# One transfer with repeated rows in place of four small ones, for the gate's second matrix in a hybrid attention step

## The chip, the cores and the metric

The kernel runs on one core of a Trainium2 chip. The metric is the device time in microseconds of one execution. The engines are called by these names: PE is TensorE (matmuls; PEld its weight loads), DVE VectorE, ACT ScalarE, POOL GpSimd, SP SyncE. A transfer (DMA) is issued by an instruction in the queue of SP or ACT; the letter q behind an engine's name in the profile (SPq, ACTq) marks such an issue.

## The reference, cut to what matters

One layer of a decoder: a prompt of 512 tokens and eight single new tokens, width 1024. One input projection gives the columns for two mixers, gated linear attention (queries, keys and values `qa`, `ka`, `va`, output gate `ga`, and the 16 columns `za` of a low-rank forget gate) and dilated window attention (`qb`, `kb`, `vb`, `gb`). What the change touches is the forget gate:

```
log_a = jax.nn.log_sigmoid((jnp.einsum('btr,rk->btk', za, w_alpha2) + b_alpha).astype(F32)) / GATE_TEMP
```

`za` has 16 columns for each token, `w_alpha2` is the gate's second matrix (16 x 256) and `b_alpha` its bias (256). The decays `log_a` then enter a recurrence over the tokens. Both mixers' outputs are gated, joined and projected by `w_out`, added to the input and normalised.

## The kernel before, in words

All products in float32 precision that feed the projections are made of three faster ones: a matrix is split into a high part (ACT copies it into a rounded type) and a low part (DVE subtracts the high part), and the matmuls high x high, high x low, low x high are added in PSUM (`three`, `split`).

The order of the work is planned on the host. Each piece of work is a generator that yields one operation at a time; the planner (`Plan.run`, line 309) takes at each step the operation that can start first by its own table of costs (`Op`, line 84), and writes it to its engine's queue (line 371, so that nearly every row of the profile has this line). Each engine then works its queue strictly in that order. A change of one operation's engine or cost therefore moves others later on. Transfers take eight semaphores in turn, whoever issues them; a transfer waits until the one that used its semaphore before has landed.

The start is this. `dense` (line 715) runs eight warm-up matmuls on PE and then the first products: for each of eight blocks `k` of 128 input columns, and for each of two halves `u` of the tokens, three groups of weights (`ka0`, `ka1`, `qa1`) times x, three matmuls each: 18 matmuls a block. `first_loads` (line 558) issues the transfers for it: x in pieces (`x_raw`) and the weights (`raw_ka`), all on SP but the first weights, which ACT issues. `first_splits` (line 587) splits what has landed: into `xx` for x and `hi_ka`, `lo_ka` for the weights. Behind the loads of x and weights stand, on SP, `zw` (the weights of `za`), `cf` (an identity matrix and other constants), the small tables `rb_raw`, `cm`, `gn`, the table `ct_raw`, and then the weights of the next groups: `raw_qa`, `raw_qb` and so on (`weight_loads`, line 524).

After the eight blocks PE forms `ps_za`, the 16 gate columns of all tokens, with the tokens in four groups of 128 (`j`), each in its own 32 rows. `gate_decay` (line 777) copies it to `zT`, adding 1 in one row of each 32 so that a bias row can be used, and multiplies with `wz`, whose 32 rows of each group hold the second matrix and the bias: products `ps_z`, of 16 matmuls. Then come the log-sigmoid (`la`) and its running sum (`b`). PE meanwhile goes on with the group `qa0`, then `qb`, `kb` and the others. `ps_tab` is one matmul of a table of biases, `ps_l` are the many small matmuls of the recurrence (three passes, lines 885 to 904), `ps_og`, `ps_s`, `ps_pt`, `ps_pv` belong to the other parts, `ps_yf` and `ps_y` are the output projection.

`wz` before: `clear` (line 543) sets it to zero on DVE, and ACT issues four transfers of 18 rows of `wab`, the 16 rows of the matrix and the bias twice, one into each group's first 18 rows. `wab` is an input of 98 rows: the matrix six times, one below the other, then the bias twice. `zw` is cleared by POOL and gets the weights of `za` in the columns 0 to 15 of its 32. The 1 is added in row 16 of each 32, so it meets the first bias row.

Of the kernel before, what the change touches and what calls it, by code (L numbers as in the profile page):

```python
# [17 lines left out]
ALU = mybir.AluOpType  # L18
AX = mybir.AxisListType
# [177 lines left out]
class Plan:  # L197
# [15 lines left out]
    def add(self, gen, prio):  # L213
        self.seq += 1
        self.tasks.append(Task(gen, prio, self.seq))

    def mark(self, name):
        self.marks[name] += 1
# [4 lines left out]
    def free(self, *xs):  # L223
        for x in xs:
            name = x.tensor.name
            self.shares[name] = self.shares.get(name, 1) - 1
            if self.shares[name] == 0:
                last = {}
                for (_, eng), end in self.uses.pop(name, {}).items():
                    last[eng] = max(last.get(eng, 0.0), end)  # L230
                tag, (pool, t, _) = self.slot_of.pop(name)
                self.slots[tag].append((pool, t, last))
# [143 lines left out]
def trunk(ctx: ExitStack, tc: tile.TileContext, xT, xp, xs, state, ck, cv, w_in, wab, gnorm,  # L376
# [6 lines left out]
    T, V, S, G, D = (plan.engines[n] for n in ("PE", "DVE", "ACT", "POOL", "SP"))  # L383
# [10 lines left out]
    def bank(tag, name):  # L394
        return Need(tag, name, [P, 512])

    def cst(name, shape, dt=F32):
        return const.tile(shape, dt, name=name)
# [34 lines left out]
    ident = cf[:, C_ID:C_ID + P]  # L433
# [90 lines left out]
    def weight_loads():  # L524
        for g in order:
            for i in range(g.parts):
                yield from g.load(i)
# [10 lines left out]
    zw = plan.alloc(Need("t1", "zw", [P, KT, 32]))  # L538
    wz = plan.alloc(Need("t1", "wz", [P, 256]))
    one16 = cst("one16", [P, 1])  # L540
    ln_eps = cst("ln_eps", [P, 1])

    def clear():

        yield V.memset(wz, 0.0)
        yield V.memset(keep, 1.0)
        yield V.memset(keep[:, CH:CH + 1], 0.0)
        yield G.memset(zw, 0.0)
        for j in range(4):
            yield S.dma_start(wz[j * 32:j * 32 + 18], wab[80:98])  # L550


    W3 = 3 * P
# [4 lines left out]
    def first_loads():  # L558
        za = w_in[:, OFF["za"]:OFF["za"] + 16].rearrange("(k p) n -> p k n", p=P)
        for n, a, *b in FIRST:  # L560
            if n == "x":
                c = b[0] if b else slice(0, NT)
                if a % 2 == 0 and c.start == 0:
                    xraw.append((yield Need("g", f"x_raw{a}", [P, 2, NT])))
                yield D.dma_start(xraw[a // 2][:, a % 2, c], xT[a * P:(a + 1) * P, c])
            else:
                if a % 2 == 0:
                    ka_raw.append((yield Need("r", f"raw_ka{a}", [P, 2, W3])))
                rows = w_in[a * P:b[0] * P, P:P + W3]
                yield (S if a == 0 else D).dma_start(ka_raw[a // 2][:, a % 2:a % 2 + b[0] - a, :], rows.rearrange("(k p) n -> p k n", p=P))  # L570
                if a == 0:
                    nc.scalar.preload_act_table_set("natural_log_exp_and_others")
            mark("first")
        yield D.dma_start(zw[:, :, :16], za)
        mark("zw")
        yield D.dma_start(cf, c_f[:, :C_E2])
        add(weight_loads(), 14.8)
        B["rb_raw"] = yield Need("t1", "rb_raw", [64, NB, HB])
        for i in range(2):
            yield D.dma_start(B["rb_raw"][i * 32:i * 32 + 32], rel_bias[:, None, :].to_broadcast([32, NB, HB]))  # L580
        yield D.dma_start(cm_w, c_m)
        mark("const")
        yield D.dma_start(gn, gnorm)
# [131 lines left out]
    def dense():  # L715
# [16 lines left out]
        for x in ka_hl:  # L732
# [6 lines left out]
                    for k in range(KT) for j in range(TT))  # L739
        free(zw, *xraw)  # L740
        add(gate_decay(pz), 5.4)
        yield from make("ka", Need("g", "ka", [P, 2, NP]), 3)
        yield from make("qa", Need("g", "qa", [P, 2, NP]), 2)
# [33 lines left out]
    def gate_decay(pz):  # L777

        zT = yield Need("t1", "zT", [P, QN[1]])
        yield At("const")  # L780

        yield V.tensor_reduce(one16, ident.rearrange("p (j r) -> p j r", r=32)[:, :, 16], axis=AX.X, op=ALU.add)
        yield V.tensor_scalar(zT[:, :P], pz[:, :P], one16, None, op0=ALU.add)
        yield V.tensor_scalar(zT[32:64, P:], pz[32:64, P:QN[1]], one16[32:64], None, op0=ALU.add)
        free(pz)
        la = yield Need("g", "la", [P, 2 * NP + 2 * NB])
        b = yield Need("g", "b", [P, 2 * NP])
        B["b"] = b
        plan.share(b, 3)
        zp = yield Pair(*(bank(("s", "t"), f"ps_z{j}") for j in range(TT)))  # L790
        yield Batch(T.matmul(zp[j][:, m * QN[1]:m * QN[1] + QN[j]], wz[j * 32:j * 32 + 32, m * P:m * P + P], zT[j * 32:j * 32 + 32, :QN[j]],
                             start=m == 0, stop=m == 1, skip_group_check=True) for m in range(2) for j in range(TT))
        free(zT, wz)
        zv = [x[:, :2 * QN[1]].rearrange("p (m t) -> p m t", m=2) for x in zp]
        lv, bv = (x[:, :2 * NP].rearrange("p (m t) -> p m t", m=2) for x in (la, b))
        ls = la[:, 2 * NP:].rearrange("p (m b) -> p m b", m=2)
        parts_ = [(zv[j][:, :, :P], lv[:, :, j * P:j * P + P], lv[:, :, j * P:j * P + P]) for j in range(TT)]
        parts_.append((zv[1][:, :, P:], ls, la_s))
        for j in (0, 1, 4, 2, 3):
            z, o, to = parts_[j]  # L800
            if j == 1:
                yield S.activation(ls, parts_[4][0], AF.Abs)
            if j != 4:
                yield S.activation(o, z, AF.Abs)
            yield S.activation(o, o, AF.Exp, scale=-1.0)
            yield S.activation(o, o, AF.Ln, bias=1.0)
            yield V.scalar_tensor_tensor(to, z, 0.0, o, op0=ALU.min, op1=ALU.subtract)
            if j == 4:
                mark("la_s")
                continue  # L810
            if j != 1:
                free(zp[j])
            for m in range(2):
                yield V.tensor_tensor_scan(bv[:, m, j * P:j * P + P], keep, lv[:, m, j * P:j * P + P], 0.0, ALU.mult, ALU.add)
        free(zp[1], la)
        mark("b")
# [830 lines left out]
    nc.vector.memset(warm, 0.0)  # L1647
    warm_ps = plan.alloc(bank("t", "warm_ps"))
    add(clear(), 0)
    add(first_loads(), 0)  # L1650
    add(first_splits(), 1)
    add(fills(), 26.3)
# [134 lines left out]
```

## Time and profile before

| | us |
|---|---|
| median of 3 runs | 282.8 |
| the three runs | 282.8, 284.8, 282.66 |
| the profiled execution | 285.62 |
| its span, first to last instruction | 283.8 |
| PE busy | 271.1 (96% of the span) |
| DVE, ACT, POOL busy | 205.6, 155.2, 57.8 |

The span is the time between the first and the last instruction of the profiled execution; the rest of its time lies around it. Busy times of PE come from modelled ends of pipelined matmuls. In a row of the timeline stand: start, length, engine, line, operation, output <- input, shape, number of instructions, and in brackets the idle time of the engine ahead of it with what ended that. In a row of the view by windows stand: the stretch, its length, the busy time of the five engines (PE, PEld, DVE, ACT, POOL) with the number of instructions in brackets, the share of the TensorE clock that was granted, the mean busy share of the 16 DMA engines, and GB/s.

### The profile page before, as it was taken

To read this page: it belongs to the slowest core of one execution; us is meant where nothing else is said; L and a number is where in the kernel's file an instruction comes from. 1 tells how busy PE (TensorE), PEld (TensorE's weight loads), DVE (VectorE), ACT (ScalarE), POOL (GpSimd) and SP (SyncE) were. 2 spreads that over 40 slices of the span, in tenths; PEclk is the share of its full clock that TensorE was granted. 3 is DMA by queue.
4 is the path that set the end of the run, shared out by engine and by line. 5 is a ranking of instruction groups with operands and counts; after the bars stand their busy time and mean duration, and the time that the engine had idled before them with its cause. 6 is when DMAs were issued, how large, how long until landed. Compare 5 with 4: busy or idle time off the path is not lost.

```text
span 283.8 us, 7076 instructions
## 1 busy us (share of the span) xinstructions
PE 271.1 (96%) x2760; PEld 254.7 (90%) x2760; DVE 205.6 (72%) x506; ACT 155.2 (55%) x449; POOL 57.8 (20%) x72
## 2 busy tenths in 40 slices
PE   4999999999989999999999999999999999999990
PEld 1999999989979999999988998999999999998890
DVE  2851689999989993619978898164989895359575
ACT  3635664536633893538878784426399955243111
POOL 4000000000397043810024182453500000000000
PEclk9799999999979999999999999999999999999997
DMA  6993654624971789833999868779883463967721
GB/s 203 308 228 75 195 164 137 161 76 123 299 247 46 205 230 262 235 132 108 308 189 199 207 170 234 201 215 233 249 212 96 147 227 88 256 124 196 229 81 74
DMA packets 59087, 52.29 MB, mean 184 GB/s; under 512 B 12509, under 2 KB 49963, under 8 KB 59053
## 3 DMA queue, kind: packets, MB, share of 16 engines
q1 hardware_dynamic: 58801, 51.56, 67.0%
q8 instruction: 22, 0.36, 0.5%
q10 hardware_dynamic: 252, 0.27, 0.3%
q14 instruction: 12, 0.10, 0.1%
HBM read 46.26 MB, written 6.03 MB: 184 GB/s over the span
## 4 chain that ended last, share of the span: by engine, by line
PE 94%; DMA 2%; DVE 1%; issue 1%; ACT 1%; DVEq 0%
PE ps_kb L371 9%; PE ps_ga L371 8%; PE ps_gb L371 8%; PE ps_qb L371 8%; PE ps_yf L371 8%; PE ps_y L371 8%; PE ps_ka L371 5%; PE ps_qa L371 4%; PE ps_vb_f L371 4%; PE ps_va_f L371 4%; PE ps_vb L371 4%; PE ps_va L371 4%; PE ps_pt L371 3%; PE ps_pv L371 3%; PE ps_s L371 3%; PE ps_l L371 2%
## 5 line engine op out<-in xcount | busy, mean ns | idle before, releaser
L371 POOL TENSOR_TENSOR past<-past,qbc 128x256 f32<-128x256 f32 x32 | 27.0, 877 | 90.9 <-DMA past<-in_ck_dram 87.6
L371 POOL TENSOR_TENSOR vv<-vv,pb 128x256 f32<-128x256 f32 x32 | 27.6, 892 | 53.7 <-DVE ms L371 26.0
L371 ACT ACTIVATE pr<-pr,ms 128x128 f32<-128x128 f32 (+3 forms) x47 | 24.4, 537 | 5.8 <-DVE ms L371 5.6
L371 DVE CUSTOM_DVE_ANT_0 pr<-ps_s,strip 128x128 f32<-128x128 f32 (+3 forms) x32 | 14.3, 479 | 6.1 <-PE ps_s L371 5.9
L371 ACT COPY pt<-ps_pt 128x256 f32<-128x256 f32 (+3 forms) x25 | 10.4, 418 | 10.1 <-PE ps_pt L371 10.0
L371 PE MATMUL ps_ka<-xx,hi_ka 128*128 128x264 f32 (+1 forms) x64 | 13.1, 297 | 2.5 <-DVE hi_ka L371 2.5
L371 PE MATMUL ps_pt<-cf,pr 128*128 128x128 f32 x80 | 14.1, 280 | 0.0
L371 ACT ACTIVATE sg<-sg 128x264 f32<-128x264 f32 (+1 forms) x32 | 13.8, 431 | 0.3
L371 PEld LDWEIGHTS ps_ka<-xx,hi_ka 128*128 128x128 f32 x64 | 10.7, 203 | 3.3 <-ACT xx L371 3.2
L371 DVE SCALAR_TENSOR_TENSOR y<-y,ps_yt 128x256 f32<-128x256 f32 x8 | 3.0, 418 | 11.3 <-PE ps_yt L371 11.3
L371 DVE TENSOR_REDUCE lt<-past 128x16 f32<-128x1024 f32 x8 | 9.7, 1209 | 1.6 <-POOL past L371 1.6
L371 DVE TENSOR_REDUCE o_pv<-vv 128x4 f32<-128x1024 f32 x8 | 9.7, 1213 | 0.5 <-POOL vv L371 0.5
L371 PEld LDWEIGHTS ps_pt<-cf,pr 128*128 128x128 f32 x80 | 9.7, 142 | 0.4 <-issue 0.3
L371 PE MATMUL ps_ka<-xx,lo_ka 128*128 128x264 f32 (+1 forms) x32 | 9.7, 302 | 0.0
L371 PE MATMUL ps_pv<-pt,v 128*64 128x256 f32 (+1 forms) x96 | 9.5, 348 | 0.0
L371 ACT COPY feat_y<-ps_yf 128x256 f32<-128x256 f32 x8 | 3.0, 373 | 11.4 <-PE ps_yf L371 11.4
L371 DVE TENSOR_SCALAR pr<-pr,ms 128x512 f32<-128x512 f32 (+3 forms) x17 | 8.9, 523 | 0.2
L371 DVE TENSOR_TENSOR xx<-x_raw,xx 128x520 fp32r<-128x520 f32 (+2 forms) x10 | 5.7, 587 | 4.3 <-ACT xx L371 4.2
L371 PEld LDWEIGHTS ps_pv<-pt,v 128*64 128x64 f32 x96 | 6.3, 137 | 2.9
L371 PE MATMUL ps_kb<-xx,hi_kb__781 128*128 128x264 f32 (+1 forms) x32 | 8.5, 336 | 0.0
L371 ACT ACTIVATE rstd<-mv,ln_eps 128x1 f32<-128x1 f32 x4 | 1.2, 291 | 13.4 <-DVE mv L371 13.4
L371 PE MATMUL ps_s<-kp,qh 64*128 64x128 f32 (+3 forms) x64 | 8.4, 346 | 0.0
(534 smaller groups left out, 1038.6 us busy)
## 6 DMA issues: line engine op xcount, KB each, us to landing
past<-in_ck_dram SPq DMA_DIRECT2D x8, 512.0 KB
vv<-in_cv_dram SPq DMA_DIRECT2D x8, 512.0 KB
pb<-psd_s SPq DMA_DIRECT2D x16, 256.0 KB
s<-in_state_dram SPq DMA_DIRECT2D x4, 512.0 KB
qbc<-qsd SPq DMA_DIRECT2D x8, 256.0 KB
strip<-tabr SPq DMA_DIRECT2D x8, 256.0 KB
y<-in_xp_dram SPq DMA_DIRECT2D x4, 512.0 KB
x_raw<-in_xT_dram SPq DMA_DIRECT2D x6, 260.0 KB
```

The costliest lines, as they stand in the source:

```text
L371: getattr(eng.eng, op.fn)(*op.args, **op.kw)
```

## The change

The four transfers on ACT and the clearing of `wz` on DVE are taken out. `wz` is filled by one transfer on SP, between those of `zw` and `cf`: the last 32 rows of `wab` (its row 66 and on), four times by a repeat of step 0, so that all 128 rows of `wz` are written. Of these 32 rows the first 14 are the matrix's rows 2 to 15, then come the whole matrix (rows 14 to 29) and the bias twice (30 and 31). So the weights of `za` now go to the columns 14 to 29 of `zw`, the columns 0 to 13, 30 and 31 stay zero, and the 1 is added in row 30. The rows of `wz` that meet zeros add nothing. What is computed is the same.

```
     def clear():
-        yield V.memset(wz, 0.0)
         yield V.memset(keep, 1.0)
         yield V.memset(keep[:, CH:CH + 1], 0.0)
         yield G.memset(zw, 0.0)
-        for j in range(4):
-            yield S.dma_start(wz[j * 32:j * 32 + 18], wab[80:98])
...
-        yield D.dma_start(zw[:, :, :16], za)
+        yield D.dma_start(zw[:, :, 14:30], za)
+        yield D.dma_start(wz, wab[None, 66:].to_broadcast([4, 32, 256]))
         mark("zw")
         yield D.dma_start(cf, c_f[:, :C_E2])
...
-        yield V.tensor_reduce(one16, ident.rearrange("p (j r) -> p j r", r=32)[:, :, 16], axis=AX.X, op=ALU.add)
+        yield V.tensor_reduce(one16, ident.rearrange("p (j r) -> p j r", r=32)[:, :, 30], axis=AX.X, op=ALU.add)
         yield V.tensor_scalar(zT[:, :P], pz[:, :P], one16, None, op0=ALU.add)
```

The queue of ACT at the start of the program, first before and then after, each with the semaphores that an instruction waits for. DMAHW0 to DMAHW7 are the eight semaphores of the transfers; `wz` is the gate's matrix, `x_raw` and `raw_ka` are x and the first weights as loaded, `xx` and `hi_ka` their split parts.

```order
L371 DMA raw_ka_109<-in_w_in_dram 128x384
L572 ACT_TABLE_LOAD
L371 DMA wz<-in_wab_dram 18x256 [waits DVE_49]
L371 DMA wz<-in_wab_dram 18x256
L371 DMA wz<-in_wab_dram 18x256 [waits DMAHW1_49]
L371 DMA wz<-in_wab_dram 18x256 [waits DMAHW3_49]
L371 CAST xx_110<-x_raw_106 128x264
```

```order
L371 DMA raw_ka_109<-in_w_in_dram 128x384
L569 ACT_TABLE_LOAD
L371 CAST xx_110<-x_raw_106 128x264 [waits DMAHW1_49]
L371 CAST xx_110<-x_raw_106 128x256 [waits DMAHW2_49]
L371 CAST xx_110<-x_raw_106 128x264 [waits DMAHW3_49]
```

The first split of x stood behind four issues, the last two of which wait for the semaphores of earlier transfers; now it is the first to wait, for the first transfer of x.

The queue of SP over the same stretch, its first loads, before and then after:

```order
L371 DMA x_raw_106<-in_xT_dram 128x256
L371 DMA raw_ka_149<-in_w_in_dram 128x384 [waits DMAHW0_49]
L371 DMA x_raw_152<-in_xT_dram 128x520 [waits DMAHW2_49]
L371 DMA raw_ka_149<-in_w_in_dram 128x384 [waits DMAHW4_49]
L371 DMA x_raw_152<-in_xT_dram 128x520 [waits DMAHW5_49]
```

```order
L371 DMA x_raw_106<-in_xT_dram 128x256
L371 DMA raw_ka_140<-in_w_in_dram 128x384
L371 DMA x_raw_146<-in_xT_dram 128x520
L371 DMA raw_ka_140<-in_w_in_dram 128x384 [waits DMAHW0_49]
L371 DMA x_raw_146<-in_xT_dram 128x520 [waits DMAHW1_49]
```

Without the four transfers the eight semaphores last longer: SP's sixth and seventh load no longer wait, and the later ones wait for earlier transfers than they did. Behind the loads, `wz` now stands on SP between `zw` and `cf`.

The queue of ACT around the split of `raw_qa`, the weights of the group `qa0`, before and then after (`rb` is the small table's copy, `tsb` the bias table's result from `ps_tab`, `ka` the first evacuated product):

```order
L371 CAST rb<-rb_raw 64x64
L371 CAST hi_qa__327<-raw_qa__227 128x1024
L371 COPY tsb<-ps_tab 8x512
L371 ACTIVATE ka<-ps_ka_137 128x256
L371 ACTIVATE ka_s<-ps_ka_137 128x8
```

```order
L371 CAST rb<-rb_raw 64x64
L371 COPY tsb<-ps_tab 8x512
L371 CAST hi_qa__315<-raw_qa__231 128x1024
L371 ACTIVATE ka<-ps_ka_132 128x256
L371 ACTIVATE ka_s<-ps_ka_132 128x8
```

The copy of `tsb` has moved ahead of the split of `raw_qa`; on PE the matmul `ps_tab` has moved with it, from the middle of the last block to its start. Further on, between the gate's product and the first pass of `ps_l`, a dozen rows of DVE and ACT stand in another order, and single rows of PE have moved by one to some twenty places; nothing else has changed.

More of the change, by code (lines that the diff above doesn't have):

```diff
@@ L543, in clear @@
     def clear():
-        yield V.memset(wz, 0.0)
         yield V.memset(keep, 1.0)
@@ L548, in clear @@
         yield G.memset(zw, 0.0)
-        for j in range(4):
-            yield S.dma_start(wz[j * 32:j * 32 + 18], wab[80:98])
     W3 = 3 * P
@@ L573, in first_loads @@
             mark("first")
-        yield D.dma_start(zw[:, :, :16], za)
+        yield D.dma_start(zw[:, :, 14:30], za)
+        yield D.dma_start(wz, wab[None, 66:].to_broadcast([4, 32, 256]))
         mark("zw")
@@ L780, in gate_decay @@
         yield At("const")
-        yield V.tensor_reduce(one16, ident.rearrange("p (j r) -> p j r", r=32)[:, :, 16], axis=AX.X, op=ALU.add)
+        yield V.tensor_reduce(one16, ident.rearrange("p (j r) -> p j r", r=32)[:, :, 30], axis=AX.X, op=ALU.add)
         yield V.tensor_scalar(zT[:, :P], pz[:, :P], one16, None, op0=ALU.add)
```

## The prediction

> **What bounds the kernel now.** I read the page of the profile first, for the engine that carries the chain that ended last.
>
> ```profile
> span 283.8 us, 7076 instructions
> PE 94%; DMA 2%; DVE 1%; issue 1%; ACT 1%; DVEq 0%
> ```
>
> TensorE carries 94% of that chain, so this change can save only where TensorE waits or runs slowly. The two small shares left, DMA and ACT, say where to look next: the first microseconds of the chain of waits, in order of time.
>
> ```profile
> 0.73 2.73 DMA x_raw<-in_xT_dram
> ...
> 3.48 2.34 DMA wz<-in_wab_dram
> 5.82 0.41 ACT xx L371
> ...
> 6.26 0.43 DVE xx L371
> 6.69 0.28 DVE hi_ka L371
> ...
> 7.11 0.48 PE ps_ka L371 x2
> ```
>
> The columns are start, length and what ran. The first tile of x lands at 0.73 + 2.73 = 3.46 us, yet its split on ScalarE begins at 5.82. Between stand 2.34 us under the name of the table `wz`, the gate's second matrix. The timeline of ScalarE and TensorE shows what this is.
>
> ```profile
> 1.19 3.42 PE L371 MATMUL warm_ps<-warm 128*128 128x512 bf16 x8 [1.19 <-DVE warm L1647]
> 3.48 0.28 ACTq L371 DMA_DIRECT2D wz<-in_wab_dram  x1
> 5.49 0.28 ACTq L371 DMA_DIRECT2D wz<-in_wab_dram  x1
> 5.81 1.03 ACT L371 CAST xx<-x_raw 128x264 fp32r<-128x264 f32 x3 [3.35 <-DMA wz<-in_wab_dram]
> 7.11 0.48 PE L371 MATMUL ps_ka<-xx,hi_ka 128*128 128x264 f32 x2 [2.50 <-DVE hi_ka L371]
> 11.15 0.41 PE L371 MATMUL ps_ka<-xx,hi_ka 128*128 128x264 f32 x2
> 13.33 0.28 PE L371 MATMUL ps_ka<-xx,hi_ka 128*128 128x264 f32 x1
> ```
>
> The four transfers themselves are small:
>
> ```profile
> wz<-in_wab_dram ACTq DMA_DIRECT2D x4, 18.0 KB
> ```
>
> The third of them is issued only at 3.48, the fourth only at 5.49. The order's rows above say why: these two wait for the DMA semaphores DMAHW1 and DMAHW3, which the transfers of x took before them (all transfers take eight semaphores in turn). ScalarE works in order, so the split of x stands behind the issue at 5.49, though its own data had come at 3.46. TensorE, after its warm-up, stands still for 2.50 us.
>
> The same rows hold a second cost. The 18 matmuls of the first block k run from 7.11 to 11.15, 4.04 us; those of the second from 11.15 to 13.33, 2.18 us. The work is equal. The view by windows has the granted clock (the column of one number after the five engines):
>
> ```profile
> 4.30:7.70 3.40, 0.88 (x5) 0.39 (x3) 1.41 (x4) 1.89 (x6) 0.00 (x0) 1.00 0.87 246
> 7.70:11.10 3.40, 3.40 (x16) 3.40 (x17) 3.34 (x8) 1.95 (x4) 0.00 (x0) 0.50 0.98 299
> 75.99:79.40 3.41, 2.09 (x124) 1.94 (x125) 2.64 (x7) 1.42 (x7) 3.33 (x4) 1.00 1.00 371
> 79.40:82.80 3.40, 3.40 (x20) 3.33 (x20) 2.91 (x6) 1.09 (x4) 3.10 (x5) 0.50 0.83 231
> ```
>
> TensorE was busy for 0.88 of 3.40 us, and the next 3.40 us were granted at 0.50. The same comes back at 79.40, behind a stretch with 2.09 busy. So a stretch of idle is paid twice here: once as idle, once as half clock afterwards.
>
> **The change part by part.**
>
> Start of TensorE. The four issues leave ScalarE. Its first split then waits for x alone and begins at 3.48, where the third issue now stands for the same semaphore, in place of 5.81: 2.33 us. Behind it come the rows 5.82 to 7.11 unchanged, since the first weights have landed by then (SyncE issues a transfer that waits for them, DMAHW0, at 3.73, a row below). TensorE starts at 7.11 - 2.33 = 4.78, against a warm-up that ends at 1.19 + 3.42 = 4.61. First term: 2.33.
>
> Clock of the first block. The idle stretch falls from 2.50 to 0.17 us, so the stretch from 4.30 to 7.70 is nearly all busy, and by the rows above the half clock should not follow. Bounds: 0 (it follows anyway) and 4.04 - 2.18 = 1.86. I take 1.86, since 3.4 - 0.2 of 3.4 us busy is nearer to the stretches at full clock than to the 0.88 and 2.09 that were punished. The Trainium skill, page "TensorE: Matmul & The Clock Gate", Part 1, says that a free-running window of about 3.4 us of activity sets the clock, half or full, so that its phase differs from run to run; the trace agrees with the length (3.40) and the two values. By that page some of the 1.86 could remain in a run whose window ends late; the case "start only" below has what that would give.
>
> Loads under the faster start. With 2.18 us a block, block 4 begins at 4.78 + 4 x 2.18 = 13.50. It needs the splits of loads that come now at these times:
>
> ```profile
> 11.80 0.83 ACT L371 CAST hi_ka<-raw_ka 128x768 fp32r<-128x768 f32 x1 [1.18 <-DMA raw_ka<-in_w_in_dram]
> 13.54 0.69 DVE L371 TENSOR_TENSOR xx<-x_raw,xx 128x520 fp32r<-128x520 f32 x1
> 15.55 0.96 DVE L371 TENSOR_TENSOR lo_ka<-raw_ka,hi_ka 128x768 fp32r<-128x768 f32 x1 [0.53 <-ACT hi_ka L371]
> ```
>
> The low part of x for block 4 is ready at 13.54 + 0.69 = 14.23, and its second matmul wants it at 13.62: a new wait of 0.61. Bounds: 0.61 and 0, for the load behind the split of 11.80 may come sooner: SyncE's sixth and seventh loads no longer wait (the order), and 4 x 18 KB less lie ahead. I take 0.61, the row as it is. Blocks 6 and 7 want the weights of 15.55 + 0.96 = 16.51 at 14.1 + 2 x 2.18 = 18.5: covered by 2 us.
>
> The sum: 2.33 + 1.86 - 0.61 = 3.58 us by the end of the blocks. `ps_tab` moves from the middle to the start of block 7 and costs TensorE the same.
>
> Does it last? Next come the gate's first product and the group `qa0`.
>
> ```profile
> 3.73 0.33 SPq L371 DMA_DIRECT2D raw_ka<-in_w_in_dram  x1
> 10.25 0.44 SPq L371 DMA_DIRECT2D zw<-in_w_in_dram  x1
> 10.74 1.48 SPq L371 DMA_DIRECT2D cf<-in_c_f_dram  x1
> 16.13 0.39 SPq L371 DMA_DIRECT2D raw_qa__227<-in_w_in_dram  x1
> 21.40 1.05 ACT L371 CAST hi_qa__327<-raw_qa__227 128x1024 fp32r<-128x1024 f32 x1 [4.17 <-DMA raw_qa__227<-in_w_in_dram]
> 22.48 1.23 DVE L371 TENSOR_TENSOR lo_qa__328<-raw_qa__227,hi_qa__327 128x1024 fp32r<-128x1024 f32 x1 [3.87 <-ACT hi_qa__327 L371]
> 28.62 0.39 PE L371 MATMUL ps_qa<-xx,hi_qa__327 128*128 128x264 f32 x1
> ```
>
> `qa0` starts at 28.62 now and would at 25.04; its last operand is ready at 22.48 + 1.23 = 23.71. That cover is 1.33 us, 4.91 before. Against it works the new transfer, issued on SyncE's queue ahead of `cf` and so ahead of `raw_qa`. Its issue lies between the 0.44 of `zw` and the 1.48 of `cf`; I take 0.44, as the row just ahead of its place. Even 1.48 leaves `qa0` only 0.15 late if nothing else moves, so I cost it at nothing; each us by which `raw_qa` lands later than the cover is lost one for one. The copy of `tsb`, now ahead of the split of `qa0` on ScalarE, waits for `ps_tab`; block 7 begins at about 14.1 + 3 x 2.18 = 20.7, so that the copy ends about as the load lands at 21.40. `wz` itself is wanted after `qa0` has begun. The cleared memset lies in VectorE's idle time before 6.26.
>
> Later the rows say that TensorE waits for little that does not move with it:
>
> ```profile
> 76.09 1.98 PE ps_l L371 x122
> 78.07 1.32 issue
> 100.00:140.00 40.00, 40.00 (x346) 37.68 (x345) 26.82 (x74) 24.63 (x68) 12.70 (x16) 1.00 0.74 213
> 140.00:200.00 60.00, 60.00 (x533) 56.17 (x532) 41.83 (x97) 37.44 (x97) 24.72 (x30) 1.00 0.86 204
> 80.00:100.00 20.00, 20.00 (x166) 19.32 (x167) 19.03 (x50) 11.96 (x41) 10.31 (x12) 0.93 0.52 149
> ```
>
> From 100 to 200 TensorE is busy throughout. VectorE is almost full from 80 to 100 (19.03 of 20), but its work there hangs on TensorE's results and starts earlier with them; the same operations stand in its queue. The rows shifted in VectorE's and ScalarE's order between 30 and 45 us are the same set before the last decay scan, so I cost them at nothing.
>
> The sum is made on the profiled execution: 285.62 us, that is its span of 283.8 and 1.8 around it; it becomes 282.0. The median of the runs is 282.8, 2.8 less; the half clock at 79.40 costs half of 3.4, 1.7 us, and may be what the run at 284.8 has over the two at 282.7 (a reading, not shown). The start is common to all, so I take the sum off the median: 282.8 - 3.6 = 279.2.
>
> **The rivals.**
>
> "Start only": the half clock still falls on the first blocks. For it: the clock answers in whole stretches. Against: only 0.17 us of idle are left. Block 4 then begins at 4.78 + 4.04 + 3 x 2.18 = 15.36, its operands are there, and the gain is 2.33: 280.5.
>
> "Late `raw_qa`": the broadcast clogs the queue. A row of the view by windows has the rate while loads stream, and one the gap into which the new transfer falls:
>
> ```profile
> 12.00:13.00 1.00, 1.00 (x11) 1.00 (x10) 0.33 (x1) 1.00 (x2) 0.00 (x0) 1.00 0.98 354
> 16.00:17.00 1.00, 1.00 (x11) 1.00 (x10) 1.00 (x2) 0.70 (x3) 0.00 (x0) 1.00 0.46 68
> ```
>
> Spread over all 16 DMA engines the 128 KB (128 rows of 256 numbers of 4 bytes) take 128/354 = 0.37 us, and would hide at 16.00, where the DMA share is 0.46. If the four-fold repeat ran on four engines, each would carry 32 KB at 354/16 = 22 GB/s: 1.48 us more ahead of `raw_qa`. With 1.48 of issue that is 2.96 against a cover of 1.33: 1.63 lost, 280.8. The Trainium skill, page "DMA: Bandwidth & Descriptors", section "Rules for kernel authors", says just this: an outermost dimension below 16, such as a leading repeat of c copies, confines a transfer to c engines. No row here shows a transfer's engines. Since the gap at 16.00 covers much of it, I give this case little.
>
> "No use": the later loads hold TensorE at each block instead, and the 2.33 come back as waits for `raw_ka`. For it: the 1.18 of waiting at 11.80. Against: loads lead by 2 us at block 6, and the waits in the blocks would have to grow by 3.58 beyond the 0.61 counted. That gives 282.8.
>
> "Half clock at `ps_l`", the one that ends slower: the stretch of small matmuls at 76.09, with 1.32 us of idle, was followed by half clock. There are three such passes; a new phase could let each be followed by one, 1.7 us a time. It decides from the third: 5.1 - 3.6 = 1.5 slower, 284.3. Against: the profiled execution shows it after one of three.
>
> **How the numbers follow.** A measurement here can tell about 1%, 2.8 us. Forecast 0.58 (278.6 to 280.5 by its bounds; 0.50 of it faster by over 1%, 0.08 within). Start only 0.17 (0.03 faster, 0.14 within). Late `raw_qa` 0.10 (0.01, 0.09). No use 0.07 (0.06 within, 0.01 slower). Half clock at `ps_l` 0.08 (0.04 within, 0.04 slower). Faster 0.54, within 0.41, slower 0.05. The range reaches from 278.2, the forecast without any wait at block 4 (4.19, 278.6) and a little below, to 282.4; it leaves out the last two cases.
>
> **What would show it.** Right: the first split of x on ScalarE at 3.5; the first `ps_ka` at about 4.8; 2.2 us for the first block and no 0.50 between 7.7 and 11.1; `qa0` at 25.0; all later groups 3 to 4 us earlier. Wrong: a first `ps_ka` still at 7; a granted clock of 0.50 over the first blocks; an idle stretch of TensorE ahead of `qa0` put down to its split; more stretches of 0.50 after `ps_l`.

## The result, and the profile after

| | before | after |
|---|---|---|
| median, us | 283.44 (7 runs) | 280.64 (7 runs) |
| ratio after to before | | 0.9887, 95% interval 0.9855 to 0.9918 |
| ratio in a later comparison (run 10) | | 0.990, interval 0.9865 to 0.9935 |
| the profiled execution, us | 285.62 | 280.33 |
| its span, us | 283.8 | 278.5 |
| PE, DVE, ACT busy, us | 271.1, 205.6, 155.2 | 268.6, 206.4, 155.0 |

The ratios leave disturbed executions out, so they need not equal the quotient of the medians. The change made the kernel faster by 1.1%, that is 2.8 us by the medians and 3.2 us by the ratio (0.0113 x 283.4); the prediction was 3.6. The ratio's interval makes it 2.3 to 4.1 us, so the time alone does not tell 3.6 from 2.8; the terms of the sum are judged by the profiles. The two profiled executions differ by 5.3 us, more than the runs do.

The shares of the chain that ended last, from the page of the profile after:

```profile
PE 89%; DVE 6%; issue 1%; DMA 1%; ACT 1%; DVEq 0%; ACTq 0%
```

DMA went from 2% to 1%: the 2.34 us under the name of `wz` are gone. DVE went from 1% to 6%, of which more below. The chain of waits in the first microseconds (start, length, what ran):

```profile
0.73 2.90 DMA x_raw<-in_xT_dram
...
3.66 0.42 ACT xx L371
...
4.10 0.43 DVE xx L371
4.54 0.28 DVE hi_ka L371
...
4.95 1.08 PE ps_ka L371 x3
```

The split of x starts when x has landed (0.73 + 2.90 = 3.63), not when the last transfer has been issued. The timeline of TensorE, the warm-up and the first products of three blocks:

```profile
1.19 3.59 PE L371 MATMUL warm_ps<-warm 128*128 128x512 bf16 x8 [1.19 <-DVE warm L1645]
4.95 0.78 PE L371 MATMUL ps_ka<-xx,hi_ka 128*128 128x264 f32 x2 [0.17 <-DVE hi_ka L371]
...
7.70 0.41 PE L371 MATMUL ps_ka<-xx,hi_ka 128*128 128x264 f32 x2
9.87 0.40 PE L371 MATMUL ps_ka<-xx,hi_ka 128*128 128x264 f32 x2
```

The idle time ahead of the first product is 0.17 us (2.50 before). The first block takes 7.70 - 4.95 = 2.75 us (4.04 before), the second 2.17. The trace's first record of the granted clock is 1.00 from 5.94 on; ahead of it the pair of matmuls at 4.95 lasts 0.78, the one at 7.70 0.41, so the first 0.99 us still ran at half clock.

Around the group `qa0`, the rows of SyncE, then of ScalarE, VectorE and TensorE:

```profile
8.91 0.73 SPq L371 DMA_DIRECT2D wz<-in_wab_dram  x1
...
14.59 0.39 SPq L371 DMA_DIRECT2D raw_qa__231<-in_w_in_dram  x1
```

```profile
21.11 0.57 ACT L371 COPY tsb<-ps_tab 8x512 f32<-8x512 f32 x1 [3.98 <-PE ps_tab L371]
21.59 1.04 ACT L371 CAST hi_qa__315<-raw_qa__231 128x1024 fp32r<-128x1024 f32 x1
22.66 1.23 DVE L371 TENSOR_TENSOR lo_qa__316<-raw_qa__231,hi_qa__315 128x1024 fp32r<-128x1024 f32 x1 [4.31 <-ACT hi_qa__315 L371]
25.15 0.52 PE L371 MATMUL ps_qa<-xx,hi_qa__315 128*128 128x264 f32 x2
```

`raw_qa` is issued at 14.59, 1.54 us earlier than before. The split of `qa0` shows no wait for it: it follows the copy of `tsb`, which waited for `ps_tab`. The last operand is ready at 22.66 + 1.23 = 23.89, and `qa0` begins at 25.15 with 1.26 us to spare: 28.62 - 25.15 = 3.47 us earlier than before.

### The profile page after: what moved, and what is told of

Same layout as the page of the kernel before. It is cut to its first block, busy times and chain, and to the rows that moved or that the text cites. A ratio compares the mean times of both kernels' runs of the same rounds, so it can differ in the third digit from the quotient of the medians.

```text
span 278.5 us, 7070 instructions
## 1 busy us (share of the span) xinstructions
PE 268.6 (96%) x2760; PEld 252.2 (91%) x2760; DVE 206.4 (74%) x505; ACT 155.0 (56%) x449; POOL 56.8 (20%) x72
## 4 chain that ended last, share of the span: by engine, by line
PE 89%; DVE 6%; issue 1%; DMA 1%; ACT 1%; DVEq 0%; ACTq 0%
PE ps_ga L371 9%; PE ps_gb L371 8%; PE ps_yf L371 8%; PE ps_qb L371 8%; PE ps_y L371 8%; PE ps_ka L371 4%; PE ps_vb_f L371 4%; PE ps_qa L371 4%; PE ps_va_f L371 4%; PE ps_kb L371 4%; PE ps_vb L371 4%; PE ps_va L371 4%; PE ps_pv L371 3%; PE ps_s L371 3%; PE ps_pt L371 3%; PE ps_oa L371 1%
## 5 line engine op out<-in xcount | busy, mean ns | idle before, releaser
L371 POOL TENSOR_TENSOR vv<-vv,pb 128x256 f32<-128x256 f32 x32 | 26.5, 858 | 52.9 <-DMA pb<-psd_s 49.6
L371 PEld LDWEIGHTS ps_ka<-xx,hi_ka 128*128 128x128 f32 x64 | 10.3, 195 | 1.1 <-ACT xx L371 1.1
L371 ACT ACTIVATE d<-d 128x512 f32<-128x512 f32 x11 | 6.6, 643 | 3.3 <-DVE d L371 3.3
```

Source lines behind the costliest of these rows:

```text
L371: getattr(eng.eng, op.fn)(*op.args, **op.kw)
```

## The experiments

The theory: ScalarE works in order, and its first split of x stood behind two issues that waited for landings; the change frees the split. What it gains is this earlier start, and half clock that no idle time causes any more. The rivals: the number of transfers or their form; the slots that they take of the eight semaphores; the memset and the layout; the planner's new order.

**1. Four transfers on SyncE in place of the one.**

```
-        yield D.dma_start(wz, wab[None, 66:].to_broadcast([4, 32, 256]))
+        for j in range(4):
+            yield D.dma_start(wz[j * 32:j * 32 + 32], wab[66:])
```

> The changed kernel, but with four transfers of 32 rows on SP at the place of the one with repeated rows. Theory (ScalarE's split of x no longer stands behind issues that wait for semaphores): the start is as in the changed kernel, first ps_ka at 4.95 us and qa0 at 25.1, with at most 0.5 more at qa0 because three more issues of 0.44 to 0.73 on SP stand ahead of raw_qa; the time is 280.6 +- 0.8, ratio to before 0.988 to 0.991. Rival (the form counts: one transfer in place of four): the four keep costing what they cost, first ps_ka near 7, ratio near 1.00.

Measured: ratio 0.9911 (0.9882 to 0.9939), at the upper end of what was expected. The timeline's first split and `qa0`:

```profile
3.78 0.89 ACT L371 CAST xx<-x_raw 128x264 fp32r<-128x264 f32 x2 [1.32 <-DMA x_raw<-in_xT_dram]
...
25.67 0.41 PE L371 MATMUL ps_qa<-xx,hi_qa__334 128*128 128x264 f32 x2
```

The one transfer with repeated rows is not what gains. `qa0` is 0.52 later than in the changed kernel, which is 0.12 from the start and the rest from the clock, which rose at 6.95 instead of 5.94.

**2. The kernel before, its four transfers on ScalarE, but issued later.**

```
+        yield At("zw", 1)
         for j in range(4):
             yield S.dma_start(wz[j * 32:j * 32 + 18], wab[80:98])
```

> The kernel before (memset, 18 rows, four transfers on ScalarE), but the four issues come only after SP's issue of zw in the planner's order, so that they stand between the splits of blocks 2 to 7. Theory: what counts is that nothing stands ahead of the first split, not which engine issues; first ps_ka at 4.95, qa0 at 25.1 to 25.6 (ScalarE pays 4 x 0.28 us of issue between its splits, one of them with a wait), ratio 0.988 to 0.992. Rival (the number of transfers or their engine counts): qa0 near 28.6, ratio 1.00.

Measured: ratio 0.9886 (0.9837 to 0.9936). The timeline:

```profile
3.64 0.89 ACT L371 CAST xx<-x_raw 128x264 fp32r<-128x264 f32 x2 [1.18 <-DMA x_raw<-in_xT_dram]
4.93 0.73 PE L371 MATMUL ps_ka<-xx,hi_ka 128*128 128x264 f32 x2
...
24.87 0.41 PE L371 MATMUL ps_qa<-xx,hi_qa__335 128*128 128x264 f32 x2
```

```profile
9.09 0.63 ACT L371 CAST xx<-x_raw 128x520 fp32r<-128x520 f32 x1
9.09 0.29 ACTq L371 DMA_DIRECT2D wz<-in_wab_dram  x1
10.46 0.83 ACT L371 CAST hi_ka<-raw_ka 128x768 fp32r<-128x768 f32 x1 [0.75 <-DMA raw_ka<-in_w_in_dram]
```

The whole gain is there with memset, 18 rows, four transfers and ScalarE as they were: only the place in the queue differs. The issue at 9.09 runs beside the split ahead of it, and the split behind it waits until 10.46 for its own weights. So it costs nothing that shows, less than the 4 x 0.28 that I had allowed.

**3. The one transfer, issued by ScalarE ahead of the first split.**

```
         yield G.memset(zw, 0.0)
+        yield S.dma_start(wz, wab[None, 66:].to_broadcast([4, 32, 256]))
...
-        yield D.dma_start(wz, wab[None, 66:].to_broadcast([4, 32, 256]))
```

> The changed kernel, but the one transfer with repeated rows is issued by ScalarE at the place where the four stood, ahead of the first split; it waits for no semaphore there. Theory: an issue of 0.28 us that waits for nothing is done long before x lands, so first ps_ka at 4.95 to 5.2, qa0 at 25.1 to 25.6, ratio 0.988 to 0.992. Rival (any transfer ahead of the split on ScalarE holds it): first ps_ka at 6 or later, ratio over 0.994. Rival (slots: each transfer that takes one of the eight semaphores early pushes the loads of x and weights back): first ps_ka early, but waits of several tenths at blocks 1 to 5 and qa0 at 26 or later.

Measured: ratio 0.989 (0.9857 to 0.9924). The timeline of ScalarE and TensorE:

```profile
1.23 1.14 ACTq L371 DMA_DIRECT2D wz<-in_wab_dram  x1
3.71 0.41 ACT L371 CAST xx<-x_raw 128x264 fp32r<-128x264 f32 x1 [1.24 <-DMA x_raw<-in_xT_dram]
...
5.00 0.78 PE L371 MATMUL ps_ka<-xx,hi_ka 128*128 128x264 f32 x2 [0.22 <-DVE hi_ka L371]
25.45 0.52 PE L371 MATMUL ps_qa<-xx,hi_qa__319 128*128 128x264 f32 x2
```

The issue takes 1.14 us, not 0.28, and still ends at 2.37, before x lands. Being on ScalarE ahead of the split is harmless; one slot taken early is harmless too.

**4. The kernel before with the changed layout.** Four transfers of 32 rows on ScalarE at the start, no memset, `zw` and the 1 as in the changed kernel.

```
-        yield D.dma_start(wz, wab[None, 66:].to_broadcast([4, 32, 256]))
...
         yield G.memset(zw, 0.0)
+        for j in range(4):
+            yield S.dma_start(wz[j * 32:j * 32 + 32], wab[66:])
```

> The kernel before in its four transfers on ScalarE at the start, but with the changed kernel's layout (32 rows each, no memset, weights of za in columns 14 to 29). Theory: memset and layout are worth nothing; first ps_ka at 7.1, qa0 at 28.6, ratio 0.998 to 1.003. Rival (the memset on VectorE or the layout gave a part): qa0 earlier by the part, ratio 0.995 or less.

Measured: ratio 0.9992 (0.9958 to 1.0026). Memset and layout are worth nothing here. The timeline has the old start:

```profile
1.20 4.76 ACTq L371 DMA_DIRECT2D wz<-in_wab_dram  x4
6.01 1.03 ACT L371 CAST xx<-x_raw 128x264 fp32r<-128x264 f32 x3 [3.55 <-DMA wz<-in_wab_dram]
7.30 0.48 PE L371 MATMUL ps_ka<-xx,hi_ka 128*128 128x264 f32 x2 [2.54 <-DVE hi_ka L371]
28.79 0.52 PE L371 MATMUL ps_qa<-xx,hi_qa__326 128*128 128x264 f32 x2
```

**5. The clock alone: before, with 16 warm-up matmuls.**

```
-N_WARM = 8
+N_WARM = 16
```

> The kernel before with 16 warm-up matmuls in place of 8, nothing else. It keeps the late split and takes away the idle time of TensorE ahead of the first product, so that the clock's part is seen alone. Theory (idle time ahead of the first blocks is paid again as half clock): first ps_ka stays at 7.1, the first block takes 2.2 to 2.5 us in place of 4.0, no 0.50 in the clock from 7.7 to 11.1, qa0 at 26.8 to 27.1 (1.5 to 1.8 earlier), ratio 0.993 to 0.996. Rival (the half clock is a matter of the first blocks themselves): qa0 at 28.6 or later, ratio 1.00.

Measured: ratio 0.990 (0.984 to 0.996). The timeline of TensorE:

```profile
1.19 5.22 PE L371 MATMUL warm_ps<-warm 128*128 128x512 bf16 x16 [1.19 <-DVE warm L1647]
7.05 0.49 PE L371 MATMUL ps_ka<-xx,hi_ka 128*128 128x264 f32 x2 [0.64 <-DVE hi_ka L371]
...
27.04 0.52 PE L371 MATMUL ps_qa<-xx,hi_qa__335 128*128 128x264 f32 x2
```

The start is the old one, the idle time is 0.64, the clock stays at 1.00 from 4.45 on, and `qa0` is 1.58 us earlier than in the profile before. So the second term is real and apart from the first. It also shows another way to a part of the gain: a warm-up that lasts until the data are there. By `qa0` that part is 1.58 of 3.47 us. The ratio is lower than the 0.993 to 0.996 expected and equal to that of the change, but its interval is wide, and these five executions do not tell the part from the whole.

**6. Its mirror: the changed kernel with 3 warm-up matmuls.**

```
-N_WARM = 8
+N_WARM = 3
```

> The changed kernel with 3 warm-up matmuls in place of 8, the mirror of the run with 16: the early split stays, an idle time of about 2.5 us ahead of the first product comes back. Theory: first ps_ka at 4.95 as in the changed kernel, half clock over the first block or more, first block 3.7 to 4.4 us, qa0 at 26.2 to 27.5 (1 to 2.3 later than in the changed kernel), ratio to before 0.992 to 0.997. Rival (the clock does not answer to this idle time): qa0 at 25.1 and the ratio of the changed kernel, 0.989.

Measured: ratio 0.9952 (0.991 to 0.9994). The timeline:

```profile
5.00 0.78 PE L371 MATMUL ps_ka<-xx,hi_ka 128*128 128x264 f32 x2 [2.36 <-ACT xx L371]
...
8.79 0.41 PE L371 MATMUL ps_ka<-xx,hi_ka 128*128 128x264 f32 x2
26.26 0.52 PE L371 MATMUL ps_qa<-xx,hi_qa__310 128*128 128x264 f32 x2
```

The early start alone keeps 2.36 us of the gain of 3.47 at `qa0` (28.62 - 26.26); by the ratio it is about half, with an interval from almost nothing to 0.9%. The first block takes 3.79 us, and the clock rises at 8.35; `qa0` is 1.11 later than in the changed kernel.

**7. Three transfers early, the fourth late.** The kernel before, but

```
-        for j in range(4):
+        for j in range(3):
             yield S.dma_start(wz[j * 32:j * 32 + 18], wab[80:98])
+        yield At("zw", 1)
+        yield S.dma_start(wz[96:114], wab[80:98])
```

> The kernel before with three of the four transfers where they were, ahead of the first split on ScalarE, and only the fourth (which waits for the third piece of x) moved behind SP's issue of zw. Theory (only the wait of the last issue costs; the third waits for the same landing as the split itself): first split at 3.7 to 3.9, first ps_ka at 5.0 to 5.3, qa0 at 25.1 to 25.8, nearly the whole gain, ratio 0.988 to 0.992. Rival (each issue costs its share of ScalarE): a quarter of the gain, qa0 near 27.7, ratio 0.997.

Measured: ratio 0.9894 (0.9838 to 0.9951), as expected. In its profile the start came later than expected, and the clock later still:

```profile
4.15 1.03 ACT L371 CAST xx<-x_raw 128x264 fp32r<-128x264 f32 x3 [1.68 <-DMA x_raw<-in_xT_dram]
...
5.44 0.78 PE L371 MATMUL ps_ka<-xx,hi_ka 128*128 128x264 f32 x2 [0.66 <-DVE hi_ka L371]
...
27.45 0.51 PE L371 MATMUL ps_qa<-xx,hi_qa__326 128*128 128x264 f32 x2
```

The chain of waits shows what stands ahead of the split:

```profile
0.73 3.07 DMA x_raw<-in_xT_dram
...
3.83 0.28 ACTq L371
```

Only the wait of the last issue had cost much: without it the split starts at 4.15. I expected 3.7 to 3.9: x landed at 0.73 + 3.07 = 3.80, which is 0.17 later than in the changed kernel, and the third issue, which waits for the same landing, took 0.28 more ahead of the split. An issue holds what stands behind it for its own length too. And `qa0` at 27.45 misses the 25.1 to 25.8 that I expected. Behind 0.66 us of idle time, half clock lasted until 10.63, past the start of the second block. The runs without a profile must have met it less often, since their ratio is that of the changed kernel; that is inferred.

**8 and 9. A version meant to beat both.** In the changed kernel the first product waits for VectorE, which makes the low part of x before it copies the first weights. Here the copy comes first (`lo_ka` and all else as before), with 6 and with 7 warm-up matmuls.

```
-N_WARM = 8
+N_WARM = 6
...
+                if j == 0:
+                    yield At("first", 2)
...
+                    yield V.tensor_copy(ka_hl[0][0][:, :1, :], ka_raw[0][:, :1, :])
                 yield from split(xraw[a // 2][:, a % 2, c], xh[a][:, c], xl[a][:, c])
...
-                    yield V.tensor_copy(hi, raw)
```

> The changed kernel, with the high part of the first weights copied on VectorE ahead of the low part of x, and 6 warm-up matmuls in place of 8: now that the start is set by x and not by ScalarE's queue, the first product could begin when both high parts are there. Theory: first ps_ka at 4.1 to 4.5 in place of 4.95, qa0 0.2 to 0.6 earlier than in the changed kernel (part of it lost, since the first matmuls run at half clock for longer), ratio to before 0.985 to 0.989. Rival (the next pieces of x and weights, or the clock, set the pace from there): qa0 as in the changed kernel or later, ratio 0.989 or more.

> The version with the high part of the first weights ahead of the low part of x, now with 7 warm-up matmuls, so that TensorE has no idle time of its own making between the warm-up and the first product (with 6 it stood for 0.30 us, and the clock rose only at 8.96). Theory (the clock rises at the end of the first stretch of 3.41 us in which TensorE was busy nearly throughout, and the phase of these stretches differs from run to run): first ps_ka at 4.2 to 4.4, clock up between 4.3 and 7.7, qa0 0.2 to 0.6 earlier than the changed kernel at an equal phase, ratio to before 0.985 to 0.988. Rival (nothing left to win at the start, the loads or the clock set the pace): ratio as for the changed kernel on the same chip or above.

Measured: 0.9869 (0.9792 to 0.9946, from three executions) with 6, and 0.9943 (0.9903 to 0.9983) with 7, beside 0.990 for the changed kernel on the latter's chip. The starts, with 6 and then with 7:

```profile
4.23 0.84 PE L371 MATMUL ps_ka<-xx,hi_ka 128*128 128x264 f32 x2 [0.30 <-DVE hi_ka L371]
26.21 0.52 PE L371 MATMUL ps_qa<-xx,hi_qa__313 128*128 128x264 f32 x2
```

```profile
4.43 0.83 PE L371 MATMUL ps_ka<-xx,hi_ka 128*128 128x264 f32 x2
24.78 0.52 PE L371 MATMUL ps_qa<-xx,hi_qa__314 128*128 128x264 f32 x2
```

The first product came 0.5 to 0.8 earlier, as expected, but the time did not follow. With 6 the clock rose only at 8.96, and `qa0` is later than in the changed kernel (in one execution, of 284.71 us, where others took 280.4). With 7 `qa0` is 0.37 earlier, and the runs show no gain for it: the expected 0.985 to 0.988 is missed. The profiled execution with 7 lost its lead near 158 us, for a reason told below under what stays open. No version here is shown to beat the change.

**10. The changed kernel again**, on the chip of run 9, unedited.

> The changed kernel once more, beside the version with another order at the start and for a second profile of it. Theory: ratio to before 0.986 to 0.992, first ps_ka at 4.9 to 5.1; qa0 between 24.8 and 26.6 by the phase of the clock's stretches, since each us by which the clock rises after 4.95 costs half a us. Rival (the gain seen first was of one chip): ratio over 0.994.

Measured: ratio 0.990 (0.9865 to 0.9935); first product at 5.02, clock up at 4.08, `qa0` at 24.98.

**11 and 12. The kernel before again**, unedited, twice, for its profile.

> The kernel before once more, for its profile alone. In seven of the ten profiles of kernels with an earlier start or no half clock, the transfers of strip (the score's bias) near 145 to 158 us came late by 0.6 to 2.9 us, in neither of the two profiles with the late start. Theory (it is chance of that transfer stage, whatever the start): such a wait of 0.5 to 3 us of VectorE for strip appears in about half of the profiles of the kernel before too, so in one or both of this and the next run. Rival (the earlier start itself runs into these transfers and loses part of the gain there): no wait for strip in either. In both: first ps_ka at 7.0 to 7.3, half clock over part of the first blocks, qa0 at 27.5 to 29.8 by the phase of the clock.

> The kernel before a third time, for its profile alone, as the run ahead of it: theory, a wait for strip of 0.5 to 3 us in one or both of the two; rival, in neither.

Measured: 283.31 and 283.58 us in one run each. There was no wait for `strip` in either, so the theory in that text did not hold; more on it below. What the two profiles show of the start was worth more. First the one, then the other:

```profile
4.86 1.03 ACT L371 CAST xx<-x_raw 128x264 fp32r<-128x264 f32 x3 [2.40 <-DMA x_raw<-in_xT_dram]
...
6.15 0.78 PE L371 MATMUL ps_ka<-xx,hi_ka 128*128 128x264 f32 x2 [1.37 <-DVE hi_ka L371]
27.72 0.52 PE L371 MATMUL ps_qa<-xx,hi_qa__327 128*128 128x264 f32 x2
```

```profile
6.53 0.78 PE L371 MATMUL ps_ka<-xx,hi_ka 128*128 128x264 f32 x2 [1.75 <-DVE hi_ka L371]
27.77 0.52 PE L371 MATMUL ps_qa<-xx,hi_qa__327 128*128 128x264 f32 x2
```

The old start is not a fixed time. The last issue waits for the third piece of x, and the split begins when that has landed and the issue's 0.28 us are over: at 4.86, 5.23, 5.81 and 6.01 us in four profiles. Expected was a first product at 7.0 to 7.3; it came at 6.15 and 6.53.

## Why the prediction was right, and where its sum was not

The numbers of all profiles that bear on the start, in us. "Clock up" is when the granted clock went to 1.00 to stay; "rest" is the time from the first product to `qa0`, less half of the part of it that ran at half clock.

| kernel | first split | first product | clock up | `qa0` | rest |
|---|---|---|---|---|---|
| before | 5.81 | 7.11 | 11.14 | 28.62 | 19.80 |
| before again (11) | 4.86 | 6.15 | 10.16 | 27.72 | 19.56 |
| before again (12) | 5.23 | 6.53 | 9.87 | 27.77 | 19.57 |
| four on ScalarE, new layout (4) | 6.01 | 7.30 | 11.43 | 28.79 | 19.78 |
| after | 3.66 | 4.95 | 5.94 | 25.15 | 19.70 |
| after again (10) | 3.73 | 5.02 | 4.08 | 24.98 | 19.96 |
| four on SyncE (1) | 3.78 | 5.07 | 6.95 | 25.67 | 19.66 |
| four on ScalarE, later (2) | 3.64 | 4.93 | 5.48 | 24.87 | 19.66 |
| one on ScalarE (3) | 3.71 | 5.00 | 6.36 | 25.45 | 19.77 |
| before, 16 warm-up (5) | 5.76 | 7.05 | 4.45 | 27.04 | 19.99 |
| after, 3 warm-up (6) | 3.71 | 5.00 | 8.35 | 26.26 | 19.58 |
| three early (7) | 4.15 | 5.44 | 10.63 | 27.45 | 19.41 |

(Before: 28.62 - 7.11 = 21.51, less half of the 3.42 from 7.72 to 11.14. After: 25.15 - 4.95 = 20.20, less half of 0.99.) The last column is 19.4 to 20.0 throughout, and 19.6 and 19.8 in runs 8 and 9. So, to within 0.6 us, two things set when `qa0` begins: the first product, and how long half clock lasts behind it. Nothing larger than that is left for what else the edits moved: the form of the transfer, the slots, the memset or the planner's order up to there. What the order does behind `qa0` was not tried apart.

- **Start, 2.33.** The mechanism is shown (runs 2, 3, 4 and 7). The size held for the pair of profiles (2.16; x itself landed 0.17 later), but not for the kernel: the mean first product of the four profiles with the late start (before, 11, 12, 4) is 6.77, of the five with the early one (after, 10, 1, 2, 3) 4.99, which makes 1.78. The step that failed is the sentence "The start is common to all, so I take the sum off the median": the landing that the last issue waits for differs by over a us from run to run.
- **Clock of the first block, 1.86.** Shown apart by runs 5 and 6. In the pair it was 4.04 - 2.75 = 1.29; over the nine profiles it is 3.00 - 1.78 = 1.22 (mean `qa0` 28.22 late, 25.22 early). I took it that 0.17 us of idle time would leave full clock throughout; in fact the clock had mostly not yet risen when the first product came, and rose up to two us after it (4.08 to 6.95).
- **New wait at block 4, 0.61.** It did not come: block 4 begins at about 14.2, and its operand is ready by 11.75 + 1.30 = 13.05:

```profile
11.75 1.30 DVE L371 TENSOR_TENSOR xx<-x_raw,xx 128x520 fp32r<-128x520 f32 x2
```

  The low part of x for block 4 was ready at 14.23 before and is ready by 13.05 now. So the lower bound of 0 was right; that the loads come sooner because SyncE waits for fewer semaphores fits this and was not tried apart. This error offset part of the two above.
- **`raw_qa`.** I costed the transfer at nothing, and it cost nothing: 1.26 us to spare. The repeat does run on four engines, by the landings in the trace: `wz` gives four, from 15.29 to 15.66, where others give sixteen, and four of the sixteen of a neighbour in the queue come at 15.52 to 16.36 when the twelve are there by 14.65. That is what the Trainium skill says on the page "DMA: Bandwidth & Descriptors", section "Rules for kernel authors"; the trace agrees, and the lag is hidden here. The rival "Late `raw_qa`" had the mechanism and not the effect.
- **"Start only".** The averaged result lies between it (2.33) and the forecast (3.58). It is no separate case but one end of a spread: the profile of run 7 has a start 1.67 earlier than before and gains 1.17 by `qa0`.
- **The sum** was made for one execution, whose start was later than usual. With the means it is 1.78 + 1.22 = 3.0, and the runs measured 2.8 to 3.2. That `qa0` came at 25.15 where 25.04 was forecast was luck: the start fell short by 0.17 and the clock by 0.57, and the wait of 0.61 that did not come made up for them.

**Does it last?** "All later groups 3 to 4 us earlier" held up to the first pass of `ps_l` (3.4), not as a uniform shift behind it. Two pieces of the chain after show what moves it:

```profile
55.09 1.00 issue
...
94.46 0.24 PE ps_vb_f L371 x2
```

At `ps_og` the stall without a visible cause is 1.00 us, where it was 0.35: the lead falls by the difference, to 2.7. At the third pass before has 1.32 us of such a stall and 3.41 us of half clock behind it; after has neither, and the lead grows to 5.9, by the starts of the same groups of TensorE. Then 0.9 are lost (`ps_vb_f` at 94.46 here was at 99.48, 5.0 later): from 72 to 89 us the chain runs over its rows (most of its 6%), and TensorE waits 0.60 us for it at 88.57.

```profile
80.00:85.00 5.00, 5.00 (x44) 5.00 (x43) 5.00 (x7) 1.86 (x5) 5.00 (x6) 1.00 0.17 68
88.57 0.43 PE L371 MATMUL ps_s<-kp,qh 64*128 64x128 f32 x3 [0.60 <-DVE ms L371]
```

VectorE is busy for all of 80 to 85. So "its work there hangs on TensorE's results and starts earlier with them" was only nearly so. Where such stalls come in the twelve other profiles they have 0.3 to 1.8 us, on both sides of the change, and half clock at `ps_l` is in none of them. I count these as what differs between executions, and not to the change.

**What stays open.** In seven of the ten profiles of kernels whose start or clock was changed, VectorE waits for a late transfer of `strip` near 156 us, by 0.6 to 3.5 us in all; the second profile of the changed kernel has it, the first does not. Its rows, in that order:

```profile
156.62 0.56 DVE L371 CUSTOM_DVE_ANT_0 pr<-ps_s,strip 128x384 f32<-128x384 f32 x1 [2.11 <-DMA strip<-tabr]
```

```profile
154.44 0.54 DVE L371 CUSTOM_DVE_ANT_0 pr<-ps_s,strip 128x384 f32<-128x384 f32 x1
```

None of the four profiles with the unchanged start has it. If it were chance at 7 in 14, none in these four would come in 35 of 1001 draws. Against a cause in the earlier start: the time between that transfer's issue and its use is the same, 10.3 us before (149.22 to 159.49) and 10.6 after (143.81 to 154.44). In the second profile of the changed kernel, which has the wait, the issue came at 145.27 and the use at 156.62, 11.3 us later. The wait reaches TensorE: in six of the seven profiles its group `ps_gb` waits 0.8 to 2.4 us for VectorE there, and in run 9 the 2.05 us of it (up to 158.44) are followed by half clock from 159.14 to 162.56. So it can cost one execution as much as the change gains. Whether the earlier start loses a part of its gain there is not settled.

## What to carry to other kernels

Read what an engine's first useful instruction stands behind in its own queue, issues of transfers included: an issue that waits for a semaphore holds the work behind it, for the wait and for its own length (0.28 us in run 7), and one that stands where the next work waits for its own data costs nothing that shows (run 2). So moving it a few places later is worth as much as moving it to another queue. Price a wait at the start by several executions, since the landing that ends it and the time when the clock rises differ from run to run. And count idle time of TensorE ahead of dense work as idle, and perhaps a second time as half clock: at the start half clock followed in the profile before and in run 4, but of four idle stretches of 1.3 to 1.8 us at `ps_l` only one was followed by it (before, 1.32; not runs 3, 4 and 8).

## What was not expected of the hardware

- The clock rose between 4.08 and 11.43 us after the span's start, in kernels that differ little. The half clock that followed idle time in a kernel already at full speed was 3.41 to 3.42 us long in all four cases (7.72 to 11.14, 8.02 to 11.43, 79.40 to 82.82, and 159.14 to 162.56 in run 9).
- How long TensorE was busy in the stretch of 3.41 us ahead of a possible change (counted back or on from a change in the same profile) does not decide it alone. At half clock, 2.75 us busy (run 7, up to 7.22) and even 3.11 (run 8, 2.14 to 5.55) left the clock at half, while 2.89 (run 10, up to 4.08) raised it. At full clock, 2.09 us busy (before, up to 79.40) brought half clock, and 2.07 (run 3, 74.63 to 78.04) did not. What else counts stays open.
- The Trainium skill, page "TensorE: Matmul & The Clock Gate", Part 1, gives a free-running window of that length and a transition that varies by 500 ns with its phase. The length agrees. The spread is wider here: in the five profiles with the early start the clock rose 2.9 to 5.8 us after TensorE's first matmul at 1.19.
- The issue of the one transfer with repeated rows took 1.14 us on ScalarE's queue (run 3) and 0.73 us on SyncE's (after); the four late ones of run 2 took 0.28 to 0.54 us each.
- The same kernel's third piece of x, one of the first transfers of all, landed so differently that the split could begin at 4.86 us in one execution (run 11) and at 5.81 in another (before).
